# Two-input element-wise work of the projection moved from GpSimd to VectorE, in a hybrid attention and gMLP block

## The chip, the cores and the metric

One NeuronCore of a Trainium2 chip runs the whole kernel. The metric is the device time of one execution in microseconds (us), as the median over several runs. Five engines work side by side, each with its own queue that it runs in order: TensorE (PE in the profile; PEld is its weight load), VectorE (DVE), ScalarE (ACT), GpSimd (POOL) and SyncE (SP), which here issues the transfers.

## The reference

One layer over 2048 latent tokens of width 1024, with 256 context tokens; all tensors are float32. Cut to what matters:

```python
h_x = modulate(x, norm1_g[l], sh1, sc1)                # RMS norm, scale and shift
p_x = h_x @ w_in[l]                                    # 1024 x 3840: the projection
k_x = apply_rope(rmsnorm(kv_heads(p_x[..., :K_W]), k_norm_g[l]), cos, sin)
v_x = kv_heads(p_x[..., K_W:KV_COLS])
q_x, u_x, vg_x, ga_x, gb_x = jnp.split(p_x[..., KV_COLS:], REST_SPLITS, axis=-1)
q_x = apply_rope(rmsnorm(q_heads(q_x), q_norm_g[l]), cos, sin) * q_scale
attn_x = merge_heads(attend_blocked(q_x, k_all, v_all))
gm_x = gmlp_spatial(jax.nn.gelu(u_x), jax.nn.gelu(vg_x), gm_norm_g[l], gm_ws[l], gm_bs[l])
x = x + g1 * branch_merge(attn_x, gm_x, ga_x, gb_x, w_br_attn[l], w_br_gm[l], w_out[l])
h2 = modulate(x, norm2_g[l], sh2, sc2)
x = x + g2 * sq_relu_mlp(h2, w_ff1[l], w_ff2[l])
```

`gmlp_spatial` normalises gelu(v) in groups of 64 columns, multiplies by the weight `gm_norm_g`, and multiplies by a 128x128 matrix per group.

## The kernel before

The kernel has four stages that follow each other on TensorE: the projection (up to about 800 us), the attention (to about 1470), the merge of the branches (to about 1850) and the MLP. The change touches the projection alone (`project`).

Each float32 operand of a matmul is split into a high part in the matmul's own type (`fp32r`) and the low remainder, and each product is three matmuls, high by high, high by low, low by high (L176, L177, L178 in `mm3`). `split` makes the two parts: the high part is a cast, on ScalarE (L144) or VectorE (L146), and the low part is a subtraction of two inputs (L148), on GpSimd or VectorE as its argument `lo_eng` says.

The 2048 tokens go in four blocks of 512 (b = 0 to 3). For each block, `w_tiles` streams the 3840 columns of `w_in` once more, in 30 chunks of 1024 elements per partition: a load by SyncE into a `w` tile (L457), the high part on ScalarE, and the low part on VectorE for the even chunks, on GpSimd for the odd ones. `w_next` keeps a list of four chunks, and the 12 `w` tiles go round. A block does in turn:

- keys and values (`kv_block`, `token_mm`; two groups of two token tiles), with the RMS norm of the heads and the rotary step (`rope`, L393 to L400);
- the queries (`q_mm`, `wide_mm`), the same with four heads at a time;
- v of the gMLP, then u, each through `gelu2`: ScalarE squares (L583), GpSimd does the one-input polynomial step (L584), VectorE multiplies (L587), ScalarE takes tanh (L588), VectorE finishes (L590) and so frees the bank of PSUM;
- `gm_v` on v, in two halves: the norm's factor on VectorE (L603), the norm's weight on GpSimd (L610), the split (L144, L148);
- 16 gates (`gate_mm`; in the profile `b<-t,w`), between which the spatial product of the gMLP stands (`gm_spatial`, `b<-t,t`).

The factors of the norms come from `rsqrt`, a chain of Newton steps on VectorE over 16 columns (L154 to L171). While the gates run, the next block's h is built: transposes on TensorE (L182), L440 on ScalarE, the cast L146 and the subtraction L148 on VectorE. For the first block there is nothing to run beside: its h comes at the head, after the context's, and there alone half of the low parts are GpSimd's (`lo=True`). During the last block's gates the first maxima of the attention are taken (TensorE L1529, VectorE L1540). PSUM has 8 banks, which go round in the order in which the program takes them.

Inside the projection a scheduler sets the order of each engine's queue, from the program's order and its own estimates. Where an instruction changes its engine, other instructions can therefore change their places.

Of the kernel before, what the change touches and what calls it, by code (L numbers as in the profile page):

```python
# [13 lines left out]
ALU = mybir.AluOpType  # L14
# [53 lines left out]
class Kern:  # L68
# [316 lines left out]
    def rope(self, tabs, src, dst, tmp, nh):  # L385
        nc = self.nc
        t1, t2 = tabs
        H = HD // 2

        def tab(t, lo, n):  # L390
            return t[:, :, lo : lo + n].unsqueeze(2).broadcast_to([P, TT, nh, n])

        nc.gpsimd.tensor_tensor(  # L393
            out=tmp[:, :, :, :H], in0=src[:, :, :, H:], in1=tab(t2, 0, H), op=ALU.mult
        )
        nc.gpsimd.tensor_tensor(
            out=tmp[:, :, :, H:], in0=src[:, :, :, :H], in1=tab(t2, H, H), op=ALU.mult
        )
        nc.vector.tensor_tensor(out=dst, in0=src, in1=tab(t1, 0, HD), op=ALU.mult)
        nc.vector.tensor_tensor(out=dst, in0=dst, in1=tmp, op=ALU.add)  # L400
# [30 lines left out]
    def h_build(self, xs, G, S, out, lo=False):  # L431
        nc = self.nc
        n = len(xs) * P
        for k in range(KC):
            hh, hl = self.t2([TB], F32R), self.t2([TB], F32R)
            out.append((hh, hl))
            ps = self.bank([TB])
            self.transposes(ps, [x[:, k * P : (k + 1) * P] for x in xs])
            tmp = self.t2([TB])
            nc.scalar.activation(  # L440
                tmp[:, :n], ps[:, :n], AF.Identity, scale=G[:, k : k + 1], bias=S[:, k : k + 1]
            )
            self.split(
                tmp[:, :n], hh[:, :n], hl[:, :n], hi_eng="dve",
                lo_eng="pool" if lo and k % 2 else "dve",
            )
            yield

    def w_tiles(self):
        w_in = self.I["w_in"][0]  # L450

        def chunk(lo, n):
            wv = w_in[:, lo : lo + n].rearrange("(k p) c -> p k c", p=P)
            a = D // n
            for i in range(KC // a):
                st = self.w4([a, n])
                self.nc.sync.dma_start(st, wv[:, a * i : a * i + a, :])  # L457
                wh, wl = self.w4([a, n], F32R), self.w4([a, n], F32R)
                self.split(st, wh, wl, lo_eng="pool" if i % 2 else "dve")
                yield [(wh[:, k, :], wl[:, k, :]) for k in range(a)]  # L460

        for b in range(NB):
            yield from chunk(0, 256)
            for c in (COL_Q, COL_VG, COL_U):
                yield from chunk(c, 512)
            for c in range(4):
                yield from chunk(COL_GA + 256 * c, 256)
                yield from chunk(COL_GB + 256 * c, 256)
# [131 lines left out]
    def gm_v(self, c, v):  # L600
        nc = self.nc
        rb = self.group_rstd(v, TT, 4, scale=0.25)
        nc.vector.tensor_tensor(out=v, in0=v, in1=rb, op=ALU.mult)  # L603
        gn = (
            self.gng[:, c * 256 : (c + 1) * 256]
            .rearrange("p (g d) -> p g d", d=HD)
            .unsqueeze(1)
            .broadcast_to([P, TT, 4, HD])
        )
        nc.gpsimd.tensor_tensor(out=v, in0=v, in1=gn, op=ALU.mult)  # L610
        vh, vl = self.t4([TT, 4, HD], F32R), self.t4([TT, 4, HD], F32R)
        self.split(v, vh, vl, lo_eng="dve")
        return vh, vl
# [1091 lines left out]
```

## Time and profile before

| | |
|---|---|
| median of 3 runs | 3123.49 us (3121.77 to 3127.06) |
| profiled execution, its time | 3121.05 us |
| its span, first to last instruction | 3119.3 us |
| TensorE busy | 3045.5 us (98%) |
| VectorE busy | 1937.7 us (62%) |
| ScalarE busy | 1352.0 us (43%) |
| GpSimd busy | 917.5 us (29%) |
| mean granted TensorE clock | 0.995 |

How to read it: times in the trace are us from the span's start. A row of the order of time gives start, length, engine, line, operation, out<-in by tile names, shapes and a count; in square brackets stands the idle time ahead of it and what ended that. A group row gives count, busy us, mean ns of one, then the idle time ahead and its releasers. A row of the waits gives who waited for whom: us in total, times, longest. A busy TensorE is a modelled figure: its matmuls are pipelined, so what counts is where it stands idle and at which clock it runs.

### The profile page before, as it was taken

The page shows a single profiled execution, that of the slowest core. Times are in us where ns is not written, and L with a number is a line of the kernel's source. Part 1 is how long each engine was busy: PE and PEld are TensorE (multiplying, and loading weights), DVE is VectorE, ACT ScalarE, POOL GpSimd, SP SyncE. Part 2 cuts the span into 40 slices and gives each one's busy share as a digit, 9 for nine tenths or more (in the row PEclk, how much of TensorE's full clock was granted, in tenths as well). Part 3 has the DMA queues.
Part 4 walks back from the last instruction along what each step waited for, and adds up shares of the span by engine and source line. Part 5 has one row for each costly group of instructions (what it writes and reads, how often), then busy time and mean ns, then how long its engine had stood idle before and what let it go on. Part 6 is the DMA issues. An engine that isn't in the chain of part 4 may idle for free.

```text
span 3119.3 us, 38046 instructions
## 1 busy us (share of the span) xinstructions
PE 3045.5 (98%) x13892; PEld 2299.1 (74%) x13892; DVE 1937.7 (62%) x2797; ACT 1352.0 (43%) x2058; POOL 917.5 (29%) x635
## 2 busy tenths in 40 slices
PE   7999999999999999999999999999999999999999
PEld 4888788877655555555777877887777788888777
DVE  4735666576677777677643478876654576654445
ACT  3353434433545454545322244444543344444433
POOL 1423324241688888888133300000000000000000
PEclk9999999999999999999999999999999999999999
DMA  6353555535100000002855448888576644445565
GB/s 202 112 177 119 200 166 172 188 93 188 38 14 5 18 11 18 11 5 91 272 161 161 151 145 314 313 306 280 190 259 204 216 149 154 158 147 194 206 215 203
DMA packets 332174, 485.42 MB, mean 156 GB/s; under 512 B 33969, under 2 KB 166321, under 8 KB 331986
## 3 DMA queue, kind: packets, MB, share of 16 engines
q1 hardware_dynamic: 324002, 478.38, 46.0%
q10 hardware_dynamic: 7984, 4.61, 0.5%
q8 instruction: 109, 1.79, 0.2%
q14 instruction: 79, 0.65, 0.1%
HBM read 348.56 MB, written 134.35 MB: 155 GB/s over the span
## 4 chain that ended last, share of the span: by engine, by line
PE 79%; DVE 7%; DMA 6%; POOL 3%; ACT 2%; issue 2%; SPq 0%; ACTq 0%; DVEq 0%; POOLq 0%
PE b L1196 12%; PE b L1197 12%; PE b L1195 11%; PE b L1597 8%; PE b L176 7%; PE b L178 7%; PE b L177 7%; PE b L1564 5%; PE b L1583 4%; PE b L1529 3%; PE b L182 2%; DMA bw<-in_w_br_gm 1%; DMA w<-in_w_in 1%; DVE f L1292 1%; DMA f<-ao_d 1%
## 5 line engine op out<-in xcount | busy, mean ns | idle before, releaser
L1292 DVE TENSOR_TENSOR f<-f,f 128x1024 fp32r<-128x1024 f32 x224 | 272.9, 1223 | 269.3 <-ACT f L1291 265.3
L1540 DVE TENSOR_REDUCE ts<-b 128x1 f32<-128x512 f32 x512 | 314.5, 681 | 172.6 <-PE b L1529 172.6
L1291 ACT CAST f<-f 128x1024 fp32r<-128x1024 f32 x224 | 235.2, 1053 | 330.8 <-DMA f<-ao_d 293.2
L1196 PE MATMUL b<-f,f 128*128 128x512 f32 x896 | 350.8, 392 | 5.1 <-DVE f L1292 4.6
L1197 PE MATMUL b<-f,f 128*128 128x512 f32 x896 | 348.9, 389 | 0.0
L1613 POOL TENSOR_TENSOR ac<-ac,p 128x512 f32<-128x512 f32 x216 | 296.3, 1403 | 70.7 <-ACT p L1587 69.5
L1195 PE MATMUL b<-f,f 128*128 128x512 f32 x896 | 306.6, 391 | 10.2 <-ACT b L1334 4.5
L1587 ACT ACTIVATE p<-b 128x512 f32<-128x512 f32 x384 | 199.6, 616 | 156.2 <-PE b L1583 153.4
L148 POOL TENSOR_TENSOR w<-w,w 128x1024 fp32r<-128x1024 f32 x60 | 148.6, 2477 | 399.5 <-ACT w L144 169.3
L1613 POOL TENSOR_TENSOR ac<-ac,t 128x512 f32<-128x512 f32 x160 | 232.5, 1478 | 0.1
L1196 PE MATMUL b<-hl,f 128*128 128x512 f32 x576 | 225.3, 391 | 2.2 <-DVE hl L971 2.1
L1195 PE MATMUL b<-hl,f 128*128 128x512 f32 x576 | 224.6, 390 | 0.0
L1197 PE MATMUL b<-hl,f 128*128 128x512 f32 x576 | 224.3, 390 | 0.0
L144 ACT CAST w<-w 128x1024 fp32r<-128x1024 f32 x120 | 125.9, 1049 | 217.4 <-DMA w<-in_w_in 181.3
L176 PE MATMUL b<-t,w 128*128 128x512 f32 x512 | 204.2, 399 | 5.7 <-DVE t L590 5.4
L1195 PEld LDWEIGHTS b<-f,f 128*128 128x128 f32 x896 | 167.5, 188 | 50.8 <-ACT f L1291 7.0
L1196 PEld LDWEIGHTS b<-f,f 128*128 128x128 f32 x896 | 168.2, 188 | 46.5 <-DVE f L1292 12.2
L178 PE MATMUL b<-t,w 128*128 128x512 f32 x512 | 200.9, 392 | 0.0
L177 PE MATMUL b<-t,w 128*128 128x512 f32 x512 | 200.5, 392 | 0.0
L1564 PE MATMUL b<-t,t 128*128 128x512 f32 x576 | 197.8, 413 | 0.8 <-ACT p L1587 0.5
L178 PE MATMUL b<-w,t 128*128 128x512 f32 (+1 forms) x528 | 192.0, 364 | 2.6 <-POOL t L148 2.5
L1197 PEld LDWEIGHTS b<-f,f 128*128 128x128 f32 x896 | 168.2, 188 | 34.4
(228 smaller groups left out, 6461.6 us busy)
## 6 DMA issues: line engine op xcount, KB each, us to landing
w<-in_w_in SPq DMA_DIRECT2D x120, 512.0 KB
ao_d<-f SPq DMA_DIRECT2D x224, 256.0 KB
f<-ao_d SPq DMA_DIRECT2D x112, 512.0 KB
f<-w2o_d SPq DMA_DIRECT2D x112, 512.0 KB
f<-in_w_ff SPq DMA_DIRECT2D x48, 1024.0 KB
w2o_d<-f SPq DMA_DIRECT2D x112, 256.0 KB
md<-in_w_mod SPq DMA_DIRECT2D x32, 512.0 KB
f<-x_d SPq DMA_DIRECT2D x64, 256.0 KB
```

The lines of the kernel that those rows point to most:

```text
L176: mm(ps, sh, mh, start=start, stop=False)
L177: mm(ps, sh, ml, start=False, stop=False)
L178: mm(ps, sl, mh, start=False, stop=stop)
L1195: mm(ps, wh, hh, start=start and k == 0, stop=False, skip_group_check=True)
L1196: mm(ps, wh, hl, start=False, stop=False, skip_group_check=True)
L1197: mm(ps, wl, hh, start=False, stop=k == len(w) - 1, skip_group_check=True)
L1291: nc.scalar.copy(h, f32(l))
L1292: nc.vector.tensor_tensor(out=l, in0=f32(l), in1=f32(h), op=ALU.subtract)
L1540: nc.vector.tensor_reduce(out=self.mx[:, t, h, c : c + 1], in_=ps[h], axis=AX.X, op=ALU.max)
L1564: self.nc.tensor.matmul(self.pts[j][h], k.KA[c][self.kv][:, ks], self.qa[h], start=True, stop=False, skip_group_check=True,)
L1597: nc.tensor.matmul(self.o[h * HD : (h + 1) * HD, :], k.V[c][:, i, self.kv * HD : (self.kv + 1) * HD], pt[h], start=j == 0, stop=j == NKT - 1,)
L1613: nc.gpsimd.tensor_tensor(out=self.acc[e][:, h], in0=old[:, h], in1=pt[h], op=ALU.add)
```

## The change

Four edits put work with two inputs from GpSimd on VectorE. All weight splits have their low part on VectorE, 60 more of them; the two rotary products L393 and L396 (12 calls, 24 instructions) go there, the norm-weight product L610 (8), and the low parts of the first block's h (4). GpSimd keeps in the projection the one-input step L584 and clearing.

```diff
-        nc.gpsimd.tensor_tensor(
+        nc.vector.tensor_tensor(
             out=tmp[:, :, :, :H], in0=src[:, :, :, H:], in1=tab(t2, 0, H), op=ALU.mult
         )
-        nc.gpsimd.tensor_tensor(
+        nc.vector.tensor_tensor(
             out=tmp[:, :, :, H:], in0=src[:, :, :, :H], in1=tab(t2, H, H), op=ALU.mult
         )
...
                 tmp[:, :n], hh[:, :n], hl[:, :n], hi_eng="dve",
-                lo_eng="pool" if lo and k % 2 else "dve",
+                lo_eng="dve",
             )
...
-                self.split(st, wh, wl, lo_eng="pool" if i % 2 else "dve")
+                self.split(st, wh, wl, lo_eng="dve")
...
-        nc.gpsimd.tensor_tensor(out=v, in0=v, in1=gn, op=ALU.mult)
+        nc.vector.tensor_tensor(out=v, in0=v, in1=gn, op=ALU.mult)
```

In the queues the change shows at three places. The first is GpSimd's queue in the last block, around the gelu of u. Names are tile kinds with a running number: `w_6045` the low part of a weight chunk, `t_1018` and `t_1019` the halves of v, `t_98` the norm's weight, `t_1074` and `t_1075` the first two token tiles of u.

```order
-L610 TENSOR_TENSOR t_1018_5676<-t_1018_5676,t_98_569 128x1024
-L148 TENSOR_TENSOR w_6045<-w_6042,w_6044 128x1024
-L610 TENSOR_TENSOR t_1019_5677<-t_1019_5677,t_98_569 128x1024
 L584 TENSOR_SCALAR t_1074_6014<-t_1074_6014 128x512
 L584 TENSOR_SCALAR t_1075_6021<-t_1075_6021 128x512
```

The three instructions ahead of the gelu step are gone from this queue, so L584 of u follows that of v directly. The second place is VectorE's queue at the same point.

```order
 L603 TENSOR_TENSOR t_1019_5677<-t_1019_5677,ts_5864 128x1024
 L148 TENSOR_TENSOR t_1047_5856<-t_1018_5676,t_1046_5855 128x1024
+L610 TENSOR_TENSOR t_1019_5677<-t_1019_5677,t_98_569 128x1024
+L148 TENSOR_TENSOR w_6045<-w_6042,w_6044 128x1024
 L587 TENSOR_TENSOR t_1074_6014<-t_1074_6014,b_5890 128x512
 L148 TENSOR_TENSOR t_1055_5885<-t_1019_5677,t_1054_5884 128x1024
```

The second norm-weight product and a weight split now stand ahead of L587 of u; the first L610 stands five instructions further up, one after the first L603. The third place is VectorE's queue at the head, where it makes the first block's h; `t_100`, `t_104` and so on are its high parts, `t_101`, `t_105` the low parts.

```order
 L359 TENSOR_SCALAR rg_q<-rg_q 128x64
+L148 TENSOR_TENSOR w_494<-w_491,w_493 128x1024
 L146 CAST t_104_590<-t_107_597 128x512
-L148 TENSOR_TENSOR w_494<-w_491,w_493 128x1024
+L148 TENSOR_TENSOR t_105_591<-t_107_597,t_104_590 128x512
 L146 CAST t_108_601<-t_111_608 128x512
 L148 TENSOR_TENSOR t_109_602<-t_111_608,t_108_601 128x512
 L146 CAST t_112_612<-t_115_619 128x512
+L148 TENSOR_TENSOR t_113_613<-t_115_619,t_112_612 128x512
```

Each cast now has its subtraction right behind it on the same engine. Further up in the same queue two weight splits (`w_476`, `w_488`) have come in. TensorE's queue changes here as well: 16 matmuls of the second key/value pair (`b_818`) stand ahead of the end of the first pair's first token tile (`b_767`), where they stood behind that pair before; nowhere else does its order change.

## The prediction

> **What bounds the kernel now.** I read the page first, then the whole projection as one stretch of the stage view (columns: length, then busy us and instructions of PE, PEld, DVE, ACT, POOL, then granted clock, DMA share, GB/s).
>
> ```profile
> span 3119.3 us, 38046 instructions
> PE 3045.5 (98%) x13892; PEld 2299.1 (74%) x13892; DVE 1937.7 (62%) x2797; ACT 1352.0 (43%) x2058; POOL 917.5 (29%) x635
> 40.00:760.00 720.00, 700.18 (x3445) 585.78 (x3444) 432.71 (x839) 297.08 (x423) 240.01 (x129) 0.99 0.50 156
> ```
>
> TensorE is the bound. In the 720 us of the projection it lacks only 19.8 us (720.0 - 700.2), VectorE is busy 60%, GpSimd 33%. So nothing that GpSimd does counts by its length; only what TensorE waits for, and any half-speed clock, can be won. The third view is TensorE's waits between 100 and 830 us (in total, times, longest).
>
> ```profile
> PE b L177 <- DVE t L148: 5.5, 2, 2.9
> PE b L176 <- DVE t L590: 5.4, 2, 4.0
> PE b L1529 <- ACT t L1504: 2.0, 1, 2.0
> ```
>
> The five rows under these hold 0.3 us or less each, and none names a weight tile: the weight splits are never waited for there. The first two rows are one stall in each of the four token blocks, 10.9 us together. The fourth view, the order of time around the stall of the last block, shows what makes it.
>
> ```profile
> 678.81 2.26 DVE L167 TENSOR_TENSOR ts<-ts,ts 128x16 f32<-128x16 f32 x1
> 681.11 2.32 DVE L168 TENSOR_SCALAR ts<-ts 128x16 f32<-128x16 f32 x1
> 683.67 1.23 DVE L603 TENSOR_TENSOR t<-t,ts 128x1024 f32<-128x1024 f32 x1
> 689.01 0.69 DVE L587 TENSOR_TENSOR t<-t,b 128x512 f32<-128x512 f32 x1 [2.98 <-POOL t L584]
> 690.76 0.74 DVE L590 SCALAR_TENSOR_TENSOR t<-t,b 128x256 f32<-128x256 f32 x2
> 678.63 2.41 POOL L610 TENSOR_TENSOR t<-t,t 128x1024 f32<-128x1024 f32 x1 [8.21 <-DVE ts L171]
> 681.00 2.39 POOL L148 TENSOR_TENSOR w<-w,w 128x1024 fp32r<-128x1024 f32 x1
> 684.98 3.30 POOL L610 TENSOR_TENSOR t<-t,t 128x1024 f32<-128x1024 f32 x1 [1.58 <-DVE t L603]
> 688.36 0.62 POOL L584 TENSOR_SCALAR t<-t 128x512 f32<-128x512 f32 x1
> 682.03 0.58 ACT L583 ACTIVATE t<-b 128x512 f32<-128x512 f32 x1
> 691.64 0.47 PE L176 MATMUL b<-t,w 128*128 128x512 f32 x1 [3.99 <-DVE t L590]
> ```
>
> Two things stand here. The gelu step L584 had its input at 682.61 (682.03 + 0.58), but began at 688.36: on GpSimd's queue it stood behind the norm-weight product L610. L587, L590 and the gate matmul that needs the bank follow it. And VectorE's Newton steps on 16 columns, which last 0.17-0.18 us elsewhere in that stretch, took 2.26 and 2.32 us, each just as long as the GpSimd instruction that had begun 0.1-0.2 us before: the two engines lock each other out. In block 2 the other form of the stall stands, and what follows both:
>
> ```profile
> 507.56 0.39 PE L177 MATMUL b<-t,t 128*128 128x256 f32 x1 [2.56 <-DVE t L148]
> 508.60:511.90 3.30, 3.30 (x12) 2.72 (x11) 1.43 (x2) 2.13 (x4) 2.26 (x3) 0.50 0.00 0
> 692.90:696.20 3.30, 3.30 (x9) 2.62 (x8) 3.20 (x7) 1.33 (x2) 1.69 (x2) 0.50 0.00 0
> 64.90:71.60 6.70, 5.67 (x24) 5.37 (x25) 5.36 (x21) 0.69 (x2) 1.70 (x2) 0.50 0.01 2
> ```
>
> The granted clock is 0.50 for about 3.3 us right after the stalls of blocks 2 and 3, and for 6.7 us at the head, where TensorE waits for h.
>
> **The change part by part.** Prices come from the groups by form:
>
> ```profile
> L148 POOL TENSOR_TENSOR w<-w,w 128x1024 fp32r<-128x1024 f32 x60 | 148.6, 2477 | 399.5 <-ACT w L144 169.3 <-PE b L178 133.4 <-PE b L276 42.9
> L148 DVE TENSOR_TENSOR w<-w,w 128x1024 fp32r<-128x1024 f32 x60 | 74.4, 1241 | 59.9 <-ACT w L144 58.6 <-PE b L177 0.8
> L610 POOL TENSOR_TENSOR t<-t,t 128x1024 f32<-128x1024 f32 x8 | 23.8, 2972 | 36.5 <-DVE ts L171 24.6 <-DVE t L603 6.5 <-DVE ts L166 5.4
> L393 POOL TENSOR_TENSOR t<-t,t 128x512 f32<-128x512 f32 x8 | 18.6, 2319 | 27.3 <-DVE t L572 14.7 <-DVE ts L166 12.7
> L396 POOL TENSOR_TENSOR t<-t,t 128x512 f32<-128x512 f32 x8 | 11.3, 1415 | 0.0
> L167 DVE TENSOR_TENSOR ts<-ts,ts 128x16 f32<-128x16 f32 x48 | 22.5, 481 | 0.1
> DVE w L148 <- ACT w L144: 57.4, 26, 9.9
> ACT w L144 <- DMA w<-in_w_in: 171.1, 55, 11.1
> ```
>
> VectorE's load. It takes 60 weight splits at 1.24 us (74.4 us), 8 products L610 at 1.23, the price of L603, which has that shape (9.8), and 28 pieces of at most 512 columns (16 + 8 of the rotary product, 4 splits of h), priced at the 0.69 us of L587 (19.3): 104 us. No row shows the strided rotary product on VectorE; its ends are nothing, if lock-outs give it back, and GpSimd's own 2.32, and 0.69 is taken since the element count is that of L587. Given back are lock-outs: L167 alone shows 48 x (0.48 - 0.18) = 14 us, and the head below 7 more. So VectorE goes from 433 us to between 500 and 537 of 720, at most 75%. It does not become the bound by load. Cover for the weight splits: their consumers stand up to four weight chunks behind in the list wq, and the lists of waits show no wait on them. If that cover went, the price would be the wait that each adds on VectorE (57.4 / 26 = 2.2 us, longest 9.9).
>
> Stalls of blocks 0 to 3. With L610 and the split off GpSimd's queue, L584 of the last block can start at 682.6, and on VectorE L610 follows L603. In the new order of VectorE's queue nine instructions stand between L603 of the first half (ended by 678.6, where GpSimd's first L610 starts on it) and L587 of u: L610 1.23, four Newton steps 0.8, L603 1.23, the split of v 1.23, L610 1.23, a weight split 1.24, together 7.0. So L587 starts at 685.6, takes 0.69, then comes the second split of v with ScalarE's step beside it (1.23), then L590 0.74: 688.3. TensorE had been idle since 687.65 (691.64 - 3.99). So 3.99 shrinks to 0.6. In blocks 1 and 2 the split that TensorE waited for no longer has L610 (2.41), its partner split and two lock-outs of 2.3 us ahead of it; it comes over 4 us earlier, against stalls of 2.9 and 2.56. Block 0 has 1.4. Sum of gains: 10.9 - 0.6 = 10.3.
>
> Half-clock stretches. With the two stalls gone their followers go: 2 x 3.3 x 0.5 = 3.3.
>
> The Trainium skill ("TensorE: Matmul & The Clock Gate", section "What's actually happening") says that the clock halves after an idle window of about 3.4 us; here a stall of 2.56 us was enough, and the one of 2.9 us in block 1 was not, so the trace decides. By the page only the 3.99 us stall would carry a half-clock stretch, and this term would be 1.7.
>
> The head. VectorE carries h to TensorE there:
>
> ```profile
> 44.62 2.07 DVE L286 SCALAR_TENSOR_TENSOR G<-G,ts 128x16 f32<-128x16 f32 x1
> 52.83 2.50 DVE L148 TENSOR_TENSOR t<-t,t 128x256 fp32r<-128x256 f32 x1
> 58.95 1.52 DVE L146 CAST t<-t 128x512 fp32r<-128x512 f32 x1
> 61.90 1.64 DVE L148 TENSOR_TENSOR t<-t,t 128x512 fp32r<-128x512 f32 x1
> 64.24 1.64 DVE L148 TENSOR_TENSOR t<-t,t 128x512 fp32r<-128x512 f32 x1
> 65.80 0.41 DVE L146 CAST t<-t 128x512 fp32r<-128x512 f32 x1
> 66.29 1.27 POOL L148 TENSOR_TENSOR t<-t,t 128x512 fp32r<-128x512 f32 x1 [0.96 <-DVE t L146]
> 53.16 0.38 PE L176 MATMUL b<-w,t 128*128 128x256 f32 x1 [0.96 <-ACT t L440]
> 59.13 1.03 PE L182 MATMUL b<-ident,m 128*128 128x128 f32 x8
> 78.42 0.42 DVE L525 COPY t<-b 128x256 f32<-128x256 f32 x1 [3.80 <-PE b L178]
> ```
>
> Each long row has a GpSimd two-input instruction beside it. Off go about 1.8 (L286), 2.1 (52.83, where 256 columns should take half of the 0.69 that 512 take), 1.1 (58.95), and 2 x 0.95: 6.9. On come two weight splits (w_476, w_488) and four h splits: 2 x 1.24 + 4 x 0.69 = 5.2. So VectorE has done its casts and all low halves 1.7 us before 66.2, at 64.5, where the last low half now ends at 67.56 on GpSimd: 3 us earlier. TensorE then has 56 matmuls left in the new order instead of 72, because 16 of the second pair are put ahead; 48 of this kind take 5.97 us (53.16 to 59.13), so 56 take 7.0: end of the key/value product at 71.5 instead of 78.4, 6.9 earlier. Bounds: 2.0, if the half-clock stretch stays and the new order brings nothing, and 7.5. I take 5.6, nearer the upper end, since four of the lock-outs are seen directly.
>
> New small waits of VectorE's longer queue: nothing to 4; I take 1.5, one stall like block 0's. Sum: 10.3 + 3.3 + 5.6 - 1.5 = 17.7. The profiled execution took 3121.05 (1.75 outside its span), 2.44 below the median of 3123.49; 17.7 off the two gives 3103.3 and 3105.8, and I forecast between them, 3104.5.
>
> **The rivals.**
> 1. *GpSimd's remaining step is locked out instead.* L584 keeps its place, and VectorE now has 96 more instructions, nearly all with two inputs, to collide with. Its row:
>
> ```profile
> L584 POOL TENSOR_SCALAR t<-t x32: 617/622/1475, 126.8 to 692.6; 128x512 f32<-128x512 f32 x32
> ```
>
> The longest is 0.85 us over the median. If the first L584 of u waits for a full 1.23 in each block, and VectorE's queue keeps L587 late too, the stalls fall by only half and the half clock stays: 5.2 + head 2 - 1.5 = 5.7 gained, 3116 to 3118, no change that can be told. For it: VectorE is fuller. Against it: L584 gains 5.7 us of start in the last block.
>
> The Trainium skill ("SBUF — State Buffer", section "Who interferes with whom") speaks for this rival: a VectorE instruction with two SBUF inputs contends with any GpSimd instruction that reads SBUF, one-input work included, and the one that starts first holds the port to its end. The rows 681.11 and 681.00 show it with the roles the other way round.
>
> 2. *Slower: the weight split blocks VectorE's queue.* On GpSimd a split that waits for its cast holds up nothing; on VectorE it holds up L587, L590 and the maxima of the last block, and with them TensorE's banks. Price: if w_6045 and its like wait the 9.9 us that the row above shows as longest, in each block, 4 x 9.9 = 39.6 against the gain of 19.2 without the small waits: 20 slower, 3141 to 3144; with half of that the two cancel. It decides when the added waits ahead of u pass about 6 us a block (25.4 in all, the gain and 6.2). Against it: the cast of that split had ended when GpSimd took the split at 681.00 with no wait shown.
>
> 3. *Nothing:* TensorE's 98% hides all, the stalls only move: 3119 to 3124. Against it: the stalls have their cause in the very instructions that move.
>
> **How the numbers follow.** What can be told from no change is about 0.2%, 6.2 us. The forecast with its smaller variants (gain over 6.2) has 0.76; rivals 1 and 3 (within 0.2%) 0.16; rival 2, 0.08. Range: low 3097 (all terms at their upper ends, 10.9 + 3.3 + 7.5 = 21.7 off 3121.05, less 2 for the clock at the head); high 3119, which takes in rival 1 and leaves rival 2 and most of rival 3 out, under 2 in 10.
>
> **What would show it.** Right: the waits L177 <- L148 and L176 <- L590 under 2 us together; clock 1.00 around 505 and 690; Newton steps at 0.18; key/value product of block 0 ended near 71; VectorE 500 to 537 us between 40 and 760. Wrong: TensorE waiting for a weight tile or for L1540, VectorE waiting several us at a weight split just before L587, or L584 near 1.2-1.8.

## The result, and the profile after

The changed kernel took 3104.44 us (median of 4 runs, 3100.98 to 3108.04) against 3123.23 (4 runs, 3121.77 to 3127.06): a ratio of 0.9938, 95% interval 0.9923 to 0.9954, so about 19 us faster. The forecast was 3104.5, in a range of 3097 to 3119. Measured once more beside other kernels the ratio was 0.9918 (0.9905 to 0.9932).

The number came out right, and the first experiments showed that its working was only half right. The projection won more than was forecast, and a loss that it had not foreseen took the surplus away. First the head of the page of the changed kernel.

```profile
span 3102.0 us, 37971 instructions
PE 3042.7 (98%) x13892; PEld 2299.5 (74%) x13892; DVE 1972.1 (64%) x2893; ACT 1356.6 (44%) x2058; POOL 704.1 (23%) x539
```

The projection as one stretch (length, then busy us of PE, PEld, DVE, ACT, POOL, then clock, DMA share, GB/s):

```profile
40.00:760.00 720.00, 715.54 (x3555) 598.03 (x3555) 476.89 (x956) 304.66 (x429) 28.61 (x35) 1.00 0.52 158
```

And all that TensorE waits for between 100 and 830 us (in total, times, longest):

```profile
PE b L1529 <- ACT t L1504: 2.0, 1, 2.0
PE b L1529 <- DVE ts L1540: 0.3, 1, 0.3
PE b L1529 <- DVE ts L1535: 0.3, 1, 0.3
```

All four stalls are gone; what is left belongs to the start of the attention (L1529). TensorE lacks 4.5 us of the 720 where it lacked 19.8. VectorE is busy 477 us, less than the 500 to 537 forecast, although it took over all the work named. The Newton step L167 is back at its own length (first row, a group: busy us, mean ns); that much the forecast had counted, and other instructions, which it had not, became shorter too (below). The other rows are in order of time (start, us).

```profile
L167 DVE TENSOR_TENSOR ts<-ts,ts 128x16 f32<-128x16 f32 x48 | 7.8, 179 | 0.0
```

```profile
63.48 0.69 DVE L148 TENSOR_TENSOR t<-t,t 128x512 fp32r<-128x512 f32 x1
72.75 0.41 DVE L525 COPY t<-b 128x256 f32<-128x256 f32 x1
633.33 0.69 DVE L393 TENSOR_TENSOR t<-t,t 128x512 f32<-128x512 f32 x1
```

Two rows are of the head: the last low half of h ends at 64.17 (worked out beforehand: 64.5), and the last of the key/value product is fetched at 72.75 instead of 78.42 (worked out: 71.5). The third is the strided rotary product on VectorE, at the 0.69 us that the prediction had to assume.

Laying TensorE's two instruction streams side by side, the changed kernel's lead at the same matmul is: 6.8 us behind the head, 9.0 before block 1's u, 12.9 before block 2's, 17.3 before block 3's, 23.1 behind it and 23.4 at the last matmul of the projection. At the start of the merge it is only 16.1, and at the end of the kernel 17.3. So some 7 us are lost between projection and merge. About 4 of them lie in the attention, and 3 of these at its end: there TensorE waits 1.63 us for ScalarE's L1587 where it waited 0.30 (first row: before), and behind it the granted clock is 0.50 for 3.3 us (1427.6 to 1430.9), as it was not before.

```profile
1446.80 0.98 PE L1564 MATMUL b<-t,t 128*128 128x512 f32 x2 [0.30 <-ACT p L1587]
1425.73 0.99 PE L1564 MATMUL b<-t,t 128*128 128x512 f32 x2 [1.63 <-ACT p L1587]
```

The rest is one wait. Here are, first for the kernel before and then for the changed one, that wait, what SyncE waited for ahead of the merge's first weight load (1375 to 1470 us; in total, times, longest), and that load.

```profile
1472.33 0.50 PE L176 MATMUL b<-in,bw 128*128 128x512 f32 x1 [1.81 <-ACT bw L144]
SPq L859 <- PE b L1564: 11.7, 1, 11.7
1458.56 0.39 SPq L859 DMA_DIRECT2D bw<-in_w_br_attn  x1
```

```profile
1456.22 0.80 PE L176 MATMUL b<-in,bw 128*128 128x512 f32 x1 [5.04 <-ACT bw L144]
SPq L859 <- PE b L1597: 25.6, 1, 25.6
1451.29 0.39 SPq L859 DMA_DIRECT2D bw<-in_w_br_attn  x1
```

Before, the first load went out 13.8 us ahead of the first merge matmul (1472.33 - 1458.56), released by a score matmul (L1564). After, it went out 4.9 us ahead of it, released by the very last value matmul of the attention (L1597). The memory map of the two built programs agrees with the rows. The tile of that load lies over two slots of the tag t2. The last reader of one of them is a score matmul in the kernel before and the last value matmul in the changed one: moving the weight splits changes the order in which t2 tiles come free, and so which tile lands in that slot. Nothing in the diff names the merge.

### The profile page after: what moved, and what is told of

Read it like the earlier page. It is cut to its first block, busy times and chain, and to the rows that moved or that the text cites. A ratio compares the mean times of both kernels' runs of the same rounds, so it can differ in the third digit from the quotient of the medians.

```text
span 3102.0 us, 37971 instructions
## 1 busy us (share of the span) xinstructions
PE 3042.7 (98%) x13892; PEld 2299.5 (74%) x13892; DVE 1972.1 (64%) x2893; ACT 1356.6 (44%) x2058; POOL 704.1 (23%) x539
## 4 chain that ended last, share of the span: by engine, by line
PE 89%; DMA 5%; DVE 3%; ACT 1%; issue 1%; POOL 1%; SPq 0%; DVEq 0%; ACTq 0%; POOLq 0%
PE b L1196 12%; PE b L1197 12%; PE b L1195 11%; PE b L176 10%; PE b L178 10%; PE b L177 10%; PE b L1597 8%; PE b L1564 5%; PE b L1583 4%; PE b L1529 3%; PE b L182 2%; DMA f<-w2o_d 1%; DMA bw<-in_w_br_gm 1%; POOL bw L148 1%; DMA f<-x_d 1%
## 5 line engine op out<-in xcount | busy, mean ns | idle before, releaser
L1197 PE MATMUL b<-f,f 128*128 128x512 f32 x896 | 349.6, 390 | 0.0
L1195 PE MATMUL b<-f,f 128*128 128x512 f32 x896 | 307.4, 392 | 10.3 <-ACT b L1334 4.7
L1587 ACT ACTIVATE p<-b 128x512 f32<-128x512 f32 x384 | 199.4, 615 | 159.3 <-PE b L1583 142.5
L1197 PE MATMUL b<-hl,f 128*128 128x512 f32 x576 | 224.0, 389 | 0.0
L148 DVE TENSOR_TENSOR w<-w,w 128x1024 fp32r<-128x1024 f32 x120 | 146.6, 1222 | 99.1 <-ACT w L144 70.6
L1564 PE MATMUL b<-t,t 128*128 128x512 f32 x576 | 198.4, 415 | 1.7 <-ACT p L1587 1.6
L1197 PEld LDWEIGHTS b<-f,f 128*128 128x128 f32 x896 | 168.5, 188 | 34.6
```

What stands on the lines that cost most here:

```text
L1195: mm(ps, wh, hh, start=start and k == 0, stop=False, skip_group_check=True)
L1197: mm(ps, wl, hh, start=False, stop=k == len(w) - 1, skip_group_check=True)
L1564: self.nc.tensor.matmul(self.pts[j][h], k.KA[c][self.kv][:, ks], self.qa[h], start=True, stop=False, skip_group_check=True,)
```

## The experiments

All were timed beside the kernel before; ratios are to it, with 95% intervals. Where a run is said to reach the end of the projection earlier, the first score matmul of the attention (L1529) is compared, which stands among the last gates; the changed kernel is 23.1 us earlier there.

**Round 1: one part at a time, and the queue taken away.** The theory then was the prediction's: the gelu step L584 stands on GpSimd's queue behind L610 and a weight split.

The splits alone:

```diff
-                lo_eng="pool" if lo and k % 2 else "dve",
+                lo_eng="dve",
...
-                self.split(st, wh, wl, lo_eng="pool" if i % 2 else "dve")
+                self.split(st, wh, wl, lo_eng="dve")
```

> Of the change only the splits: the low halves of the weights (L459) and of h (L445) on VectorE; the norm-weight product L610 and the rotary products stay on GpSimd. Queue theory (the four stalls of the projection come from what stands ahead of the gelu step L584 on GpSimd's queue): L610 still stands there, so of the 10.9 us about 7 go, with both half-clock stretches (3.3); the head gains its 6.7 here and nowhere else, since all its collisions are splits; the end of the projection comes about 16 us earlier. Slot theory of what is lost later (the first merge weights' load takes the memory of a buffer that the last value product reads): this edit moves that buffer, so 6 to 8 us of it are lost between attention and merge, TensorE's gap there is 5 us instead of 1.8, and the kernel takes about 3112 to 3115. Rival (the loss after attention is the same wait put off, a debt of the faster projection whatever made it): the same loss here, and also in the next kernels in proportion to what they win.

Measured 0.9931 (0.9917 to 0.9945), 3105.31 us, where 3112 to 3115 was expected: as much as the whole change. The projection ends 22.1 us earlier. All four stalls but 0.5 us are gone, more than the 7 expected, the head's gain is whole, and the merge's wait is there:

```profile
PE b L177 <- DVE t L148: 0.5, 1, 0.5
72.42 0.41 DVE L525 COPY t<-b 128x256 f32<-128x256 f32 x1
1459.88 0.80 PE L176 MATMUL b<-in,bw 128*128 128x512 f32 x1 [5.10 <-ACT bw L144]
```

The norm-weight product alone:

```diff
-        nc.gpsimd.tensor_tensor(out=v, in0=v, in1=gn, op=ALU.mult)
+        nc.vector.tensor_tensor(out=v, in0=v, in1=gn, op=ALU.mult)
```

> Of the change only the norm-weight product L610 on VectorE; all splits and rotary products stay. Queue theory: the largest part of the stalls goes (8 to 10 of 10.9 us, the half-clock stretches with them), the head keeps its loss; projection's end 10 to 13 us earlier. Slot theory: the first merge weights keep the buffer of before, so nothing is lost after attention, and 3110 to 3113 is measured. Lock-out theory (the stalls come from Newton steps that GpSimd's two-input work slows, of whatever source): L610 is only 24 of GpSimd's 200 us of two-input work in the projection, so a small part goes, 2 to 4 us, 3119 to 3121.

Measured 0.9982 (0.9972 to 0.9991), 5.6 us: half of what the queue theory asked. The lock-out theory's 2 to 4 us lie within the interval (2.8 to 8.8 us). Stalls of 2.05, 2.05 and 2.8 us stay, though L584 has no L610 ahead of it any more:

```profile
PE b L177 <- DVE t L148: 4.1, 2, 2.1
PE b L176 <- DVE t L590: 2.8, 1, 2.8
```

The rotary products alone:

```diff
-        nc.gpsimd.tensor_tensor(
+        nc.vector.tensor_tensor(
             out=tmp[:, :, :, :H], in0=src[:, :, :, H:], in1=tab(t2, 0, H), op=ALU.mult
         )
-        nc.gpsimd.tensor_tensor(
+        nc.vector.tensor_tensor(
             out=tmp[:, :, :, H:], in0=src[:, :, :, :H], in1=tab(t2, H, H), op=ALU.mult
         )
```

> Of the change only the two rotary products L393 and L396 on VectorE. Queue theory: they stand in the queue well before the stalls, so the stalls stay within 1 us in all and the time is 3122 to 3125. Lock-out theory: about 30 us of GpSimd's two-input work is gone and some of the stalls with it, 2 to 4 us, 3119 to 3121.

Measured 0.9948 (0.9936 to 0.9961), 16 us, where neither theory gave more than 4. With L610 and the weight splits still on GpSimd, three stalls are gone and the fourth is 1.0 us. The head is unchanged, and the merge's wait is the 1.8 us of before, as the slot theory says for a kernel whose weight splits stay. The waits of VectorE between 100 and 760 us say where it came from; the first two rows are the kernel before, the third this one, in which the wait for L396 doesn't occur.

```profile
DVE t L587 <- POOL t L584: 22.7, 11, 3.0
DVE t L400 <- POOL t L396: 15.4, 11, 2.4
```

```profile
DVE t L587 <- POOL t L584: 2.1, 4, 0.5
PE b L176 <- DVE t L590: 1.0, 1, 1.0
1461.17 0.50 PE L176 MATMUL b<-in,bw 128*128 128x512 f32 x1 [1.80 <-ACT bw L144]
```

The gelu step on VectorE, which the change does not do:

```diff
-        nc.gpsimd.tensor_scalar(
+        nc.vector.tensor_scalar(
             out=z, in0=z, scalar1=GELU_A, scalar2=1.0, op0=ALU.mult, op1=ALU.add
         )
```

> The kernel before with one edit that the change does not have: the gelu step L584 on VectorE, nothing else. Queue theory: the stalls in which TensorE waits for L590 (blocks 0 and 3, 1.4 and 4.0 us) go, and with the latter its half-clock stretch (1.7); the stalls in which it waits for the split of v (blocks 1 and 2, 2.9 and 2.6) stay, as L610 and the lock-outs before it stay. 5 to 7 us earlier at the end of the projection, 3116 to 3119. Lock-out theory: what makes L587 late is the norm chain, not L584, so all four stalls stay and 32 more instructions on VectorE make them a little longer: 3123 to 3127.

Measured 1.0018 (1.0008 to 1.0029), slower, as the lock-out theory had it. L584 stood behind nothing on GpSimd's queue any more, and the stall of block 3 was still 4.1 us. The rows of VectorE and GpSimd there, at v's gelu and at u's:

```profile
662.52 2.62 DVE L584 TENSOR_SCALAR t<-t 128x512 f32<-128x512 f32 x1
665.85 0.42 DVE L584 TENSOR_SCALAR t<-t 128x512 f32<-128x512 f32 x1
690.78 3.07 DVE L584 TENSOR_SCALAR t<-t 128x512 f32<-128x512 f32 x1
661.48 3.38 POOL L148 TENSOR_TENSOR w<-w,w 128x1024 fp32r<-128x1024 f32 x1
689.81 3.30 POOL L610 TENSOR_TENSOR t<-t,t 128x1024 f32<-128x1024 f32 x1 [1.37 <-DVE t L603]
```

The same step lasts 0.42 us alone, and 2.62 and 3.07 when a GpSimd instruction has begun 1 us before; it ends 0.3 and 0.7 us after that one. So the queue is one form of a more general price: a step of the chain that comes after a long two-input instruction of GpSimd waits for its end, on GpSimd's queue as well as on VectorE. The Trainium skill ("SBUF — State Buffer", section "Who interferes with whom") says that whichever of the two engines issues first holds the ports that they share for its whole instruction while the other is blocked entirely, and that a one-input step of VectorE takes part in this when it runs in a two-port mode. These rows (2.62 and 3.07 us in place of 0.42) agree on the blocking; in which mode VectorE ran, no trace shows.

The four runs together gave a new theory. In each token block a chain runs through both engines: q's first eviction (L569), norm, rotary products, v's gelu, v's norm and split, u's first gelu output (L590), which frees the bank that TensorE needs. Its steps are joined partly by their data and partly by the order of VectorE's queue. In block 3 of the kernel before it took 690.76 - 630.52 = 60.24 us and the stall was 3.99, so TensorE can do without it for 56.25. (In block 0 it is 60.5 by the same subtraction, 158.07 - 96.13 - 1.40. In blocks 1 and 2 TensorE waits for v's split, an earlier step of the same chain.) The rows of five kernels (before, norm weight, rotary, splits, changed):

```profile
630.52 0.42 DVE L569 COPY t<-b 128x256 f32<-128x256 f32 x1 [2.71 <-PE b L178]
```

```profile
628.06 0.42 DVE L569 COPY t<-b 128x256 f32<-128x256 f32 x1 [2.55 <-PE b L178]
687.09 1.41 DVE L590 SCALAR_TENSOR_TENSOR t<-t,b 128x256 f32<-128x256 f32 x4
```

```profile
620.95 0.42 DVE L569 COPY t<-b 128x256 f32<-128x256 f32 x1 [3.16 <-PE b L178]
678.16 0.75 DVE L590 SCALAR_TENSOR_TENSOR t<-t,b 128x256 f32<-128x256 f32 x2
```

```profile
613.71 0.42 DVE L569 COPY t<-b 128x256 f32<-128x256 f32 x1 [0.31 <-PE b L178]
670.02 1.45 DVE L590 SCALAR_TENSOR_TENSOR t<-t,b 128x256 f32<-128x256 f32 x4
```

```profile
613.24 0.42 DVE L569 COPY t<-b 128x256 f32<-128x256 f32 x1 [4.21 <-PE b L178]
662.87 0.74 DVE L590 SCALAR_TENSOR_TENSOR t<-t,b 128x256 f32<-128x256 f32 x2
```

| kernel, block 3 | chain, us | beyond 56.25 | stall measured | VectorE waits for GpSimd | VectorE's instructions longer by |
|---|---|---|---|---|---|
| before | 60.24 | 3.99 (sets the 56.25) | 3.99 | 10.1 | 8.3 |
| norm weight alone | 59.03 | 2.78 | 2.78 | 7.1 | 7.0 |
| rotary alone | 57.21 | 0.96 | 0.96 | 0.5 | 9.1 |
| splits alone | 56.31 | 0.06 | none | 4.2 | 6.3 |
| norm weight and rotary (below) | 54.20 | -2.05 | none | 0.5 | 8.1 |
| changed | 49.63 | -6.62 | none | 0 | 1.5 |
| splits twice (below) | 63.31 | 7.06 | 7.05 | 3.0 | 5.6 |
| gelu step alone | 61.18 | 4.93 | 4.10, and 0.61 shortly before it | 3.7 | 13.2 |

A stall is what the chain is longer than its cover, so single edits don't add: past 56.25 a shorter chain only makes slack. That the third and fourth columns agree is no test of the cause: TensorE does the same work in the meantime, so the difference has to be the stall. What made the chain long stand in the last two columns: what VectorE waited for results of GpSimd, and by how much its own instructions in the chain were longer than the shortest of the same form in that trace. The rotary products won by the waits alone (10.1 to 0.5 us, the instructions became longer); the gelu step on VectorE lost in length (4.9) most of what it saved in waits (6.4), and added its own work; the whole change took away both, and VectorE's own work in the chain, which grew from 39.6 to 51.3 us at those shortest times, went where it had waited. (Two expectations below measure to the end of the first L590, 0.4 us later: 60.65 and 56.7.)

**Round 2: the loss at the merge.** The changed kernel, unedited, for comparison on one chip:

> The changed kernel as it is, once more beside the next three, so that they are compared on one chip. Its ratio to the kernel before was 0.9938 (0.9923 to 0.9954), about 3104; the same is expected, 0.992 to 0.996. TensorE's gap at the start of the merge is 5.0 us, with half clock for 6.8 us behind it.

Measured 0.9918 (0.9905 to 0.9932); the wait was 5.54 us. Then the changed kernel with the weights of the first two merge steps put where tiles lie that the attention has read earlier (br_raw and br_weights take the tag as an argument):

```diff
-        early = [(s, self.br_raw(s[1])) for s in (next(it), next(it))]
+        early = [(s, self.br_raw(s[1], "y")) for s in (next(it), next(it))]
...
-            q.append((self.br_weights(raw, "dve"), self.gate_in(*s)))
+            q.append((self.br_weights(raw, "dve", "y"), self.gate_in(*s)))
```

> The changed kernel with the weights of the first two merge steps put into tiles of the tag y in place of bw. These lie where the t4 tiles lay, which the attention reads for the last time well before its last value product; nothing is computed otherwise. Slot theory (5.0 us of TensorE's gap and the half clock behind it come from the memory that the first weight load waits for): the load starts 25 us earlier, the gap goes below 1 us, the 6.8 us of half clock (worth 3.4) go, 6 to 8 us are won on the changed kernel: about 3096 to 3098. Rival (debt: the merge's inputs, casts or evictions are late by themselves and the loss is only put off): the gap stays over 3 us with another releaser, or comes back within the first merge steps, and under 2 us are won.

```profile
1423.29 0.54 SPq L859 DMA_DIRECT2D y<-in_w_br_attn  x1
1448.76 0.50 PE L176 MATMUL b<-in,y 128*128 128x512 f32 x1 [1.75 <-ACT y L144]
1450.67 0.63 PE L176 MATMUL b<-in,y 128*128 128x512 f32 x1
1486.84 0.50 PE L176 MATMUL b<-in,bw 128*128 128x512 f32 x1 [2.01 <-ACT bw L144]
```

The merge from 1485 us as one stretch:

```profile
1485.00:1505.00 20.00, 18.16 (x72) 14.59 (x73) 14.11 (x20) 8.70 (x15) 5.45 (x4) 0.91 0.93 312
```

Measured 0.9919 (0.9905 to 0.9932): no gain that can be told (medians 3101.91 and 3103.22). The load goes out at 1423.29 and the wait falls from 5.54 to 1.75 us, so the memory was the cause of the long wait, and the merge starts 23.6 us ahead of the kernel before in place of 17.3. But some 380 us later, at the first L1197, the leads are 20.1 and 19.2: of 6.3 us 5.4 are lost again, 3.7 of it by 1520 us, in the wait of 2.0 us for a later weight tile and the half clock behind it (0.91 over 20 us), at a DMA share of 0.93; from there on the difference goes up and down by 2 to 4 us. The debt rival was right about the time, the slot theory about the wait. Whether the transfers' bandwidth or the order of SyncE's queue sets the pace of these merge steps stays open.

The same edit on the kernel before:

> The kernel before with the same edit of the merge weights. Slot theory: there the first load waits for a tile that is read earlier, the gap is 1.8 us with no half clock behind it, so 1 to 2 us are to be won: 3121 to 3122, a ratio of 0.9993 to 0.9998. Rival (debt): nothing, or as much as in the changed kernel.

Measured 1.0002 (0.9993 to 1.0011): the wait stayed at 1.75 us, as in the changed kernel, with ScalarE's cast named in both. There the memory was no limit, and the expected 1 to 2 us were not there.

And on the kernel with the splits alone:

> Only the splits on VectorE (as in the first experiment), with the edit of the merge weights. Chain theory, formed from the first four runs: in each token block a chain over VectorE and GpSimd runs from q's eviction to u's first gelu output (L590); TensorE needs that 56.7 us after the eviction, and a stall is what goes beyond. In block 3 it came at 60.65 before, 59.45 with the norm-weight product moved, 57.63 with the rotary products, 56.74 with the splits, 50.03 with all. So the splits alone already bring the stalls to nothing, and the other two edits only add slack: this kernel is within 3 us of the changed one with the handover mended, 3096 to 3101. Rival (each edit is worth what it won alone, 5.6 us for the norm-weight product and 16 for the rotary products): 8 us or more slower than the changed kernel with the handover mended.

Measured 0.9927 (0.9914 to 0.9941), 4.3 us behind the changed kernel with the same edit (medians 3106.18 and 3101.91), slightly over the 3 expected and half of what the rival asked; the intervals overlap. In block 0 it keeps a stall of 0.96 us.

**Round 3: the chain put to the test.**

The norm-weight product and the rotary products on VectorE (the two diffs above), splits as before:

> The norm-weight product and the rotary products on VectorE, all splits as in the kernel before. Chain theory (a stall is what u's first gelu output comes later than 56.7 us after q's eviction): alone the two edits took 1.2 and 3.0 us off the 60.65 of block 3, together they give about 56.4, so the four stalls are gone and no more is won than the last 1.0 us beyond the rotary products alone; the head keeps its loss; end of the projection 15 to 17 us earlier, ratio 0.9940 to 0.9955. Additive rival (each edit is worth what it measured alone): 5.6 + 16.2 us, a ratio of 0.9925 to 0.9935.

```profile
621.47 0.42 DVE L569 COPY t<-b 128x256 f32<-128x256 f32 x1 [3.15 <-PE b L178]
675.67 0.74 DVE L590 SCALAR_TENSOR_TENSOR t<-t,b 128x256 f32<-128x256 f32 x2
79.87 0.42 DVE L525 COPY t<-b 128x256 f32<-128x256 f32 x1 [3.79 <-PE b L178]
```

Measured 0.9938 (0.9924 to 0.9951), between the two expectations. The profile decides: no stall, the end of the projection 14.9 us earlier, against 14.2 with the rotary products alone and 5.3 with the norm weight alone, so the two don't add; and the head (79.87) keeps all its loss. The chain itself was 2 us shorter than the sum of the two edits had it.

The changed kernel with L584 on VectorE (the diff above):

> The changed kernel with the gelu step L584 on VectorE too, so that GpSimd has next to nothing to do in the projection. Chain theory: u's first gelu output already comes 6.6 us before TensorE needs it, so nothing is won: within 0.15% of the changed kernel, ratio 0.990 to 0.9935, VectorE some 10 us busier between 40 and 760 us. First rival of the prediction (the 7.2 us by which L584 is held up by VectorE cost time): 3 to 6 us faster than the changed kernel.

```profile
40.00:760.00 720.00, 715.15 (x3555) 598.00 (x3552) 483.48 (x990) 305.39 (x430) 1.58 (x3) 1.00 0.52 158
```

Measured 0.9924 (0.9911 to 0.9937), no difference from the changed kernel. GpSimd is idle and VectorE has 6.6 us more; TensorE's busy time is the same to 0.4 us. So the prediction's first rival, the step locked out on GpSimd, costs nothing here that can be told.

The changed kernel with every second low half computed once more by GpSimd:

```diff
                 self.split(st, wh, wl, lo_eng="dve")
+                if i % 2:
+                    self.nc.gpsimd.tensor_tensor(out=wl, in0=st, in1=f32(wh), op=ALU.subtract)
```

> The changed kernel, in which GpSimd computes the low half of every second weight tile once more into the same tile after VectorE (60 times 2.4 us, off every path of before; the result is the same). VectorE has no less to do than in the changed kernel; only the neighbour's two-input work is back. Collision theory (what costs is a two-input instruction of GpSimd running at the time of a step of the chain, on either engine): most of the head's 6.7 us comes back, VectorE's excess over its fastest times rises from 9 to over 30 us in the projection, and u's first gelu output comes 2 to 6 us later in each block, which the 6.6 us of slack cover: 4 to 8 us slower than the changed kernel, ratio 0.993 to 0.9945. Rival (what cost was that VectorE waited for products which GpSimd computes slowly, and not the collisions): no product is waited for here, so within 2 us of the changed kernel.

```profile
L167 DVE TENSOR_TENSOR ts<-ts,ts 128x16 f32<-128x16 f32 x48 | 21.5, 454 | 0.0
687.79 2.33 DVE L167 TENSOR_TENSOR ts<-ts,ts 128x16 f32<-128x16 f32 x1
667.85 0.69 DVE L589 TENSOR_TENSOR t<-t,b 128x512 f32<-128x512 f32 x1 [2.99 <-POOL t L586]
686.87 3.21 POOL L461 TENSOR_TENSOR w<-w,w 128x1024 fp32r<-128x1024 f32 x1 [9.15 <-DVE w L148]
663.86 3.25 POOL L461 TENSOR_TENSOR w<-w,w 128x1024 fp32r<-128x1024 f32 x1 [11.62 <-DVE w L148]
633.93 0.42 DVE L571 COPY t<-b 128x256 f32<-128x256 f32 x1 [3.66 <-PE b L178]
697.24 2.06 DVE L592 SCALAR_TENSOR_TENSOR t<-t,b 128x256 f32<-128x256 f32 x6
80.58 0.41 DVE L527 COPY t<-b 128x256 f32<-128x256 f32 x1
```

(Lines behind the edit are two higher: L571 is L569, L589 is L587, L592 is L590.) Measured 1.0019 (1.0010 to 1.0027): the whole gain gone, and more, by 60 instructions on an engine that has time for them. (The profiled execution is the slowest of its twelve, 3138.31 us against a median of 3132.43.) Both forms of the price are there: a Newton step of 2.33 us beside a split that began 0.9 us before, and v's gelu step behind a split on GpSimd's queue. The head's loss is back (80.58), and the stalls are 1.28, 3.21, 3.20 and 7.05 us. The expectation had the sign and the mechanism, not the size (4 to 8 us): it let the slack of 6.6 us cover the collisions, and the chain grew by 13.7. Part of that is no collision. Against the changed kernel VectorE waits 3.0 us more for GpSimd in it and 3.2 more for ScalarE, its instructions are 4.1 longer, and 2.0 are more work of its own that the order in the queue puts ahead of u's first L590. Nor are the 60 off every path: the stall of 1.28 us is TensorE waiting for the second writing of a weight tile. Over the projection VectorE's time above its shortest forms is 56 us, where the changed kernel has 8.

Both small edits on the changed kernel:

> The changed kernel with both the gelu step L584 on VectorE and the first merge weights in tiles of y. By the chain theory the first brings nothing and by the handover run the second moves the start of the merge 6 us forward, of which 4 to 5 are lost again in the next 60 us: 1 to 2 us better than the changed kernel, ratio 0.9905 to 0.993, not to be told from it. Rival (the two small gains seen in the profiles add up): a ratio under 0.9905.

Measured 0.9923 (0.9909 to 0.9936). No version was found that is faster than the changed kernel by more than the runs differ.

## Why the prediction was right or wrong

- **TensorE is the bound, and only its waits and clock can be won.** Right: its lack in the projection fell by 15.3 us, and VectorE's 44 us more cost nothing.
- **Stalls, 10.3 us.** The sum was nearly right (all 10.9 went), the cause only partly. The step that failed is the working of block 3: it began at v's norm and counted what stands between L603 and L590, which left a stall of 0.6. The chain begins at q's eviction. Its first half, with VectorE's waits for the rotary products (15.4 us over the four blocks) and for L584 (22.7, v's and u's together), was priced at nothing but instruction time, and moving the products alone proved to be worth 16 us. After the change there are 6.6 us of slack, not 0.6 of stall. The prediction's two causes, the queue and the collisions, are not the whole: with L584 off the queue but on VectorE (the gelu step alone) collisions took the place of the wait and nothing was won, and the rotary products won their 16 us by waits that went, since VectorE's time above its shortest forms did not fall there (64 us against 58).
- **Half clock, 3.3 us.** Right: the clock is 1.00 over the projection, and in the two streams the lead grows by 1.7 and 1.6 us behind the stalls of blocks 2 and 3. So the half clock after the 2.56 us stall was real, and the trace was the better guide than the idle window of about 3.4 us of the Trainium skill ("TensorE: Matmul & The Clock Gate", section "What's actually happening").
- **Head, 5.6 us.** The key/value product came 5.7 us earlier, and TensorE's lead at the same matmul behind it was 6.8, near the 6.9 of the working. 1.4 of it are there before the first key/value matmul, which comes at 50.9 to 52.7 us in the profiles whose splits are on VectorE alone and at 53.1 to 55.4 in those where GpSimd computes any. The gain hangs on the splits alone: 79.87 with only the other edits made, 72.42 with only the splits.
- **New small waits, -1.5.** None appeared. Instead the four blocks won some 2 us beyond the listed stalls and the half clock (23.1 - 6.8 = 16.3 against 10.9 + 3.3), in pieces that no row of the waits shows.
- **VectorE at 500 to 537 us.** Wrong: 477. The 104 us of new work were fair, but what is given back was put at 21, and nearly 60 came back (433 + 104 - 477). Summed over all of VectorE's instructions, the time above the shortest of the same form fell from 58 us to 8. The prediction counted L167 and the head and left out the rest.
- **What was not in the sum:** 23.4 us were won by the last matmul of the projection against 17.7, and 6.1 of them were gone at the end. The part that is one wait (5.0 in place of 1.8 us, and the half clock behind it) comes from a tile that changed its slot. Removing that wait won nothing that could be told, so the merge would have taken most of it back in any case. The attention's share varies between 0.7 and 5.0 us from profile to profile, and is 2.1 in the kernel with the gelu step alone, which came to it late. It is 4.0 or more in just the three profiles that have a half-clock stretch behind the last wait for L1587; why the stretch comes in these isn't known. That the total came out within 0.1 us is luck: these two errors cancel, and measured again the gain was about 25 us in place of 19.
- **The rivals.** Collisions with L584 (rival 1) exist: its mean is 0.845 us against a shortest of 0.620. But it was 0.801 in the kernel before, and they cost nothing that can be told, as the changed kernel with L584 on VectorE shows. A weight split that blocks VectorE's queue (rival 2) waits 69 us in total before casts, and TensorE waits for none of it. No change (rival 3) is excluded by the interval.

## What to carry to other kernels

When TensorE waits for a result of a chain over VectorE and GpSimd, measure the chain from its first input to that result, and the time that TensorE can do without it; a stall is the difference, gains up to it count in full and beyond it not at all. Price a two-input instruction of GpSimd by what waits for it and by what it stops on VectorE, not by its own length: here 60 of them that computed nothing new undid the whole change, in part by collisions. And when an edit changes the order in which tiles come free, look at the first loads of later stages too: what they wait for may change though nothing there was edited.

## What the hardware showed that was not expected

A one-input step with constants (L584, 128x512) is blocked on VectorE just as a two-input one: 2.62 and 3.07 us in place of 0.42. The 16-column Newton steps, one-input or two-input, last 2.3 us when they fall beside a GpSimd instruction of 2.4. The half clock is not tied to a length of stall: 1.75 us at the start of the merge brought it in the changed kernel with the merge weights in tiles of y (the row of 0.63 us), and 2.56 us in block 2 of the kernel before, while 1.81 and 2.94 us there did not.
